# mLSTM of a hybrid encoder block: blocks of 128 tokens with a carried state in place of full 512x512 products

## The chip, the core and the metric

The kernel runs on one core of a Trainium2 chip, as one launch. The metric is the device time in microseconds (us). The engines have short names throughout: PE is TensorE (matrix products; PEld are its weight loads), ACT is ScalarE, DVE is VectorE, POOL is GpSimd, SP is SyncE, which issues most of the DMAs. SBUF is the working memory of 128 partitions; PSUM holds the results of PE in banks of 128 x 512 fp32.

## What is computed

The reference is one layer of an encoder on 512 tokens of width 1024, fp32 throughout. A normalised input goes through one wide projection; three mixers work on it (a bidirectional mLSTM, a 2-D neighbourhood attention, a cross-attention into 256 memory tokens), are merged by gates, projected and followed by a convolutional gated feed-forward network. The change concerns the mLSTM: 4 heads of 128 channels, run forwards and backwards and summed. Per direction the reference takes chunks of 64 tokens; inside a chunk it forms weighted scores, and between chunks it carries a state:

```python
C_new = decay[..., None, None] * C + jnp.einsum('bhl,bhld,bhle->bhde', wt, v_c, k_c)
n_new = decay[..., None] * n + jnp.einsum('bhl,bhle->bhe', wt, k_c)
...
P = jnp.exp(D - m_j[..., None]) * qk
inter_w = jnp.exp(inter_log - m_j)
num = jnp.einsum('bhcjs,bhcsd->bhcjd', P, v) + inter_w[..., None] * jnp.einsum('bhcde,bhcje->bhcjd', C_prev, q)
den = jnp.sum(P, axis=-1) + inter_w * jnp.einsum('bhce,bhcje->bhcj', n_prev, q)
h = num / jnp.maximum(jnp.abs(den), jnp.exp(-m_j))[..., None]
```

The size of a chunk is free in exact arithmetic: one chunk of 512 tokens without a state, and four chunks of 128 with one, give the same h. So do the stabilising maxima m, whatever they are, as long as they are used consistently.

## The kernel before

**Products.** Most products are done in a split form: an fp32 operand is cut into a high half (a copy in the type fp32r, by ACT) and a low half (the difference, by DVE), and `mm3` (lines 205 to 207) adds high x high, high x low and low x high. Weights arrive from DRAM as blocks of 512 KB on the SP queue, three blocks ahead, and are cut (`emit_split`, lines 187 and 188) one block ahead of their use. A few products, among them the mLSTM's values (line 603), take fp32 operands as they are; the text calls these unsplit.

**Order of the work.** The program is written against a framework of tiles: buffers come from pools of fixed size, and the framework places the semaphores and the order of each engine's queue, in which a later instruction can stand ahead of an earlier one. The main line is a row of projections (`proj`: 24 products of 512 columns for one 128-wide slice). The three mixers are written as generators; after each projection `step` lets the first unfinished one advance by 1.4 pieces on average in this part (0.75 in the projections of the memory tokens), so that a mixer's pieces stand between projections. PSUM has 4 banks for projections (`mmps`) and 4 for the mixers (`atps`).

**The mLSTM.** The queries and keys come out of a convolution (`conv`) and an activation (`silu2`, lines 398 to 403) and are cut into halves (`split_act`, lines 211 and 212) for use in `mm3`. `va` holds the values of all tokens and heads with a 129th column of constants, which yields the denominator. `ml_prep` works out the gates: cumulated log forget gates restarting at each block of 128 tokens (the scans), the running maximum m for each token and direction, `em` = exp(-m) (line 548), and `bi` (lines 550 to 558), the logarithmic weight of each source token relative to each later block, from the total decay `tot` of the blocks between. `R` (line 569, by DMA, spread to all partitions) holds the target's part; POOL adds the causal mask for the diagonal blocks (`rm`, line 572).

Per head `ml_all` then does:

- `kq_part` for each of four source blocks s: the scores of 128 source tokens to all 512 targets by `mm3`, and a copy into SBUF by ACT (line 581);
- `weights_J` for each of four target blocks J: five exponentials of 128x128 on ACT (line 591), for forward sources s = 0..J and backward sources s = J..3, and two products with the scores on DVE (lines 592 and 593);
- `values_J`: five unsplit products of the weights with `va` (line 603) into two columns groups of one PSUM bank, forward and backward; then the division by the denominator (lines 605 to 610) and the sum of squares (line 612);
- `normalise` and `emit_y`: the norm of the head, four transposes (line 627), the output gate, and a cut into halves for the branch's projection.

A piece ends at each `yield`: six per head. Values of block J-1 stand behind the weights of block J, values of block 3 in the next head's pieces.

The diff's functions stand here in full:

Of the kernel before, what the change touches and what calls it, by code (L numbers as in the profile page):

```python
# [11 lines left out]
F32 = mybir.dt.float32  # L12
# [92 lines left out]
def hybrid_block(ctx, tc, xg, xT, memT, wflat, vecs, gbias, nabias, outa, outb):  # L105
# [376 lines left out]
    def ml_prep():  # L482
        gv = Gt.rearrange("p t (d k h) -> p t d k h", d=2, k=2)
        T4 = lambda a: a.rearrange("p (t d h) -> p t d h", t=4, d=2)
        f = tiny(32)
        V.tensor_copy(T4(f), gv[:, :, :, 1, :])
        af = tiny(32)
        V.scalar_tensor_tensor(af, f, -1.0, f, op0=ALU.mult, op1=ALU.max)
        e = tiny(32)
        A.activation(e, af, AF.Exp, scale=-1.0)  # L490
        r = tiny(32)
        V.tensor_scalar(r, e, 2.0, None, op0=ALU.add)
        V.reciprocal(r, r)
# [48 lines left out]
        pmv = pm[:, :400].rearrange("p (t c) -> p t c", t=NT)  # L542
        for t in range(NT):
            PE.transpose(pmv[:, t, :], mr[:100, t * P:(t + 1) * P], ident[:100, :100])
# [3 lines left out]
        A.activation(em, pmv[:, :, 0:36], AF.Exp, scale=-1.0)  # L548
        tot = cp.tile([P, 4, 2, 4], F32, name="tot")
        V.tensor_copy(tot.rearrange("p t d h -> p (t d h)"), pt[:, :32])  # L550
        bi = cp.tile([P, 2, 4, 4, 4], F32, name="bi")
        for d in range(2):
            V.tensor_tensor(bi[:, d, 0], gv[:, :, d, 0, :], pmv[:, :, 64 + 32 * d:68 + 32 * d], op=ALU.subtract)
            for k in range(1, 4):
                if d == 0:
                    V.tensor_tensor(bi[:, 0, k, 0:4 - k], bi[:, 0, k - 1, 0:4 - k], tot[:, k - 1:3, 0, :], op=ALU.add)
                else:
                    V.tensor_tensor(bi[:, 1, k, k:4], bi[:, 1, k - 1, k:4], tot[:, 1:5 - k, 1, :], op=ALU.add)
        ml.update(rd=rd, em=em, bi=bi)

    def ml_all():
        yield from ml_prep()
        rd, em, bi = ml["rd"], ml["em"], ml["bi"]

        def load_R(h):
            R, rm = [], []
# [7 lines left out]
                rm.append(t)  # L574
            return R, rm

        def kq_part(h, kq, s):
            ps = atps()
            ks, qs = slice(h * S + s * P, h * S + (s + 1) * P), slice(h * S, (h + 1) * S)
            mm3(ps, kT[0][:, ks], kT[1][:, ks], qT[0][:, qs], qT[1][:, qs], True, True)  # L580
            A.activation(kq[:, s, :], ps, AF.Copy)

        def slots(J):
            return [(0, s) for s in range(J + 1)] + [(1, s) for s in range(J, NT)]

        def weights_J(h, J, R, rm, kq):
            js = slice(J * P, (J + 1) * P)
            E = tp.tile([P, 5, P], F32, tag="E", name=nm("E"))
            for i, (d, s) in enumerate(slots(J)):
                src = (rm if s == J else R)[d][:, js]  # L590
                A.activation(E[:, i, :], src, AF.Exp, bias=bi[:, d, abs(J - s), s, h:h + 1])  # L591
            V.tensor_tensor(E[:, 0:J + 1, :], E[:, 0:J + 1, :], kq[:, 0:J + 1, js], op=ALU.mult)
            V.tensor_tensor(E[:, J + 1:5, :], E[:, J + 1:5, :], kq[:, J:4, js], op=ALU.mult)
            return E

        def values_J(h, J, E, H, ss):
            js = slice(J * P, (J + 1) * P)
            ps = atps()
            pv = ps[:, :260].rearrange("p (d c) -> p d c", d=2)
            for d in range(2):  # L600
                lst = [(i, s) for i, (dd, s) in enumerate(slots(J)) if dd == d]
                for n, (i, s) in enumerate(lst):
                    PE.matmul(pv[:, d, 0:129], E[:, i, :], va[:, s, h, 0:129], start=n == 0, stop=n == len(lst) - 1)  # L603
# [32 lines left out]
        E = None  # L636
        R, rm = load_R(0)
        for h in range(4):
            kq = unit()[:, :4 * S].rearrange("p (s j) -> p s j", s=4)
            for s in range(2):  # L640
                kq_part(h, kq, s)
            yield
            if prev:
                values_J(h - 1, 3, E, *prev)
                normalise(*prev)
            for s in range(2, 4):
                kq_part(h, kq, s)
            yield
            H = tp.tile([P, S], F32, tag="H", name=nm("H"), bufs=4)
            ss = tiny(4)  # L650
            E = weights_J(h, 0, R, rm, kq)
            yield
            for J in range(1, NT):
                E2 = weights_J(h, J, R, rm, kq)
                if J == 3 and h < 3:
                    R, rm = load_R(h + 1)
                values_J(h, J - 1, E, H, ss)
# [5 lines left out]
        values_J(3, 3, E, *prev)  # L663
        normalise(*prev)
        yield
        emit_y(3, prev[0])
# [3 lines left out]
    def na_all(nq, nk, vw0, yh, yl):  # L670
# [55 lines left out]
        def transposes(i, sm):  # L726
# [3 lines left out]

            pp = []
            for bl in range(2):
                w = tp.tile([P, 5, P], F32R, tag="E", name=nm("w")).rearrange("p a b -> p (a b)")
# [3 lines left out]
                V.tensor_tensor(wv[:, :, 1, :], src, wv[:, :, 0, :].bitcast(F32), op=ALU.subtract)  # L737
                pp.append(w)
# [554 lines left out]
```

## Time and profile before

| what | value |
|---|---|
| median of 3 runs | 902.88 us (902.57 to 904.7) |
| the profiled execution's own time | 903.37 us |
| its span in the trace | 901.6 us |
| busy: PE, DVE, ACT, POOL | 894.5, 597.0, 466.9, 157.3 us |
| granted clock of PE, mean | 0.998 |
| instructions | 12452 |

All durations in the text come from the one profiled execution. Its span runs from the first to the last instruction in the trace; its own time is 1.8 us longer. In the listings a line begins with the source line (L603), the engine, the operation, "out<-in" by tile names, partitions x elements and a count; then come busy time and mean duration of one, and idle time of the engine before it with what ended it. A PE duration includes the time until its result has landed and overlaps with its successor's; what one product takes of PE is read from start to start, or from the chain of work that ended last, which has "start, us, what" in each row. Operands in fp32r are shown as f32. The mLSTM's pieces lie from about 108 to 255 us.

### The profile page before, as it was taken

What the parts mean: (1) busy time and instruction counts of PE and PEld (TensorE: products, weight loads), DVE (VectorE), ACT (ScalarE), POOL (GpSimd) and SP (SyncE); (2) the same over time, 40 slices, a digit from 0 to 9 for tenths busy, and PEclk for the clock granted to TensorE, in tenths of its full rate; (3) what the DMA queues carried; (4) which work ended last, traced back from release to release, by engine and by line L of the source; (5) the groups of instructions that cost most, each with busy time, mean ns of one, the idle gap of its engine ahead of it and who ended that gap; (6) DMA issues with size and microseconds to landing.
All of it is one profiled execution on the core that took longest, in us unless ns stands there. A gap on an engine that the chain in (4) does not pass through costs nothing.

```text
span 901.6 us, 12452 instructions
## 1 busy us (share of the span) xinstructions
PE 894.5 (99%) x4442; PEld 748.8 (83%) x4442; DVE 597.0 (66%) x1138; ACT 466.9 (52%) x983; POOL 157.3 (17%) x236
## 2 busy tenths in 40 slices
PE   9999999999999999999999999999999999999997
PEld 7899888888888888888888888888888888888887
DVE  6795676746666757998766547777733477777433
ACT  7474456656544647898734435444422344444442
POOL 5101231102070660420000211111100011111010
PEclk9999999999999999999999999999999999999999
DMA  7224633422252443443323422222232322222412
GB/s 263 101 72 134 200 135 97 162 93 94 71 138 74 116 126 121 136 134 118 117 89 107 144 97 96 94 97 96 65 98 95 117 95 94 94 93 89 129 41 94
DMA packets 39293, 99.69 MB, mean 111 GB/s; under 512 B 5688, under 2 KB 13624, under 8 KB 39232
## 3 DMA queue, kind: packets, MB, share of 16 engines
q1 hardware_dynamic: 31584, 92.39, 30.5%
q0 software_dynamic: 7360, 6.32, 3.2%
q8 instruction: 35, 0.57, 0.3%
q14 instruction: 26, 0.21, 0.1%
q10 hardware_dynamic: 288, 0.20, 0.1%
HBM read 94.67 MB, written 4.21 MB: 110 GB/s over the span
## 4 chain that ended last, share of the span: by engine, by line
PE 97%; ACT 1%; DMA 1%; issue 1%; SPq 0%; DVE 0%; POOLq 0%; POOL 0%; DVEq 0%
PE mm L205 28%; PE mm L207 28%; PE mm L206 28%; PE at L205 2%; PE at L206 2%; PE at L207 2%; PE at L603 2%; PE at L748 1%; PE at L729 1%; DMA wr<-wflat 1%; PE at L836 0%; PE at L711 0%; PE at L710 0%; ACT s L720 0%; PE at L290 0%
## 5 line engine op out<-in xcount | busy, mean ns | idle before, releaser
L205 PE MATMUL mm<-u,wh 128*128 128x512 f32 (+1 forms) x1076 | 419.8, 390 | 0.6 <-ACT wh L187 0.6
L206 PE MATMUL mm<-u,wh 128*128 128x512 f32 (+1 forms) x1076 | 417.4, 388 | 0.0
L207 PE MATMUL mm<-u,wl 128*128 128x512 f32 (+1 forms) x1076 | 416.9, 387 | 0.0
L187 ACT ACTIVATE wh<-wr 128x512 fp32r<-128x512 f32 (+1 forms) x298 | 186.0, 625 | 254.7 <-PE mm L206 214.0
L188 DVE TENSOR_TENSOR wl<-wr,wh 128x512 fp32r<-128x512 f32 (+3 forms) x299 | 229.6, 769 | 112.4 <-ACT wh L187 106.4
L207 PEld LDWEIGHTS mm<-u,wl 128*128 128x128 f32 x1076 | 202.1, 188 | 44.7 <-DVE wl L188 0.4
L205 PEld LDWEIGHTS mm<-u,wh 128*128 128x128 f32 x1076 | 202.1, 188 | 44.2 <-ACT wh L187 1.2
L206 PEld LDWEIGHTS mm<-u,wh 128*128 128x128 f32 x1076 | 202.3, 188 | 42.5 <-DVE u L212 0.3
L1162 POOL TENSOR_TENSOR s<-s,rb 128x512 f32<-128x512 f32 x22 | 29.2, 1328 | 266.9 <-DVE s L1161 258.8
L475 POOL DMA_DIRECT2D u<-nav_d x128 | 62.3, 503 | 75.0 <-PE at L748 34.1
L211 ACT ACTIVATE u<-s 128x512 fp32r<-128x512 f32 x34 | 21.5, 632 | 53.4 <-DVE s L1165 51.0
L212 DVE SCALAR_TENSOR_TENSOR u<-s,u 128x512 fp32r<-128x512 f32 x34 | 23.5, 692 | 14.9 <-ACT u L211 14.6
L1010 POOL TENSOR_TENSOR acc<-acc,s 128x512 f32<-128x512 f32 x7 | 9.1, 1300 | 129.7 <-ACT s L1009 129.7
L591 ACT ACTIVATE E<-R,bi 128x128 f32<-128x128 f32 x80 | 28.1, 396 | 5.6 <-POOL R L572 5.6
L393 ACT ACTIVATE s<-pad,vec 128x512 f32<-128x512 f32 x30 | 24.4, 815 | 8.3 <-DVE pad L391 8.3
L394 DVE SCALAR_TENSOR_TENSOR s<-pad,vec,s 128x512 f32<-128x512 f32 x30 | 22.5, 751 | 6.2 <-ACT s L393 6.1
L205 PE MATMUL mm<-wh,u 128*128 128x256 f32 (+1 forms) x80 | 24.5, 307 | 0.0
L206 PE MATMUL mm<-wl,u 128*128 128x256 f32 (+1 forms) x80 | 24.3, 304 | 0.0
L207 PE MATMUL mm<-wh,u 128*128 128x256 f32 (+1 forms) x80 | 24.3, 303 | 0.0
L1161 DVE SCALAR_TENSOR_TENSOR s<-s,s 128x512 f32<-128x512 f32 x22 | 15.2, 692 | 13.4 <-ACT s L1160 13.3
L391 DVE TENSOR_TENSOR pad<-mm,rb 128x512 f32<-128x512 f32 x22 | 15.1, 692 | 12.2 <-PE mm L207 12.2
L395 DVE SCALAR_TENSOR_TENSOR s<-pad,vec,s 128x512 f32<-128x512 f32 x30 | 22.5, 751 | 0.7
(282 smaller groups left out, 1049.7 us busy)
## 6 DMA issues: line engine op xcount, KB each, us to landing
wr<-wflat SPq DMA_DIRECT2D x140, 512.0 KB, 3.3
nab<-nabias SPq DMA_DIRECT2D x16, 256.0 KB, 2.7
u<-nav_d POOLq DMA_DIRECT2D x128, 32.0 KB, 2.6
s<-xT SPq DMA_DIRECT2D x15, 256.0 KB, 4.0
wr<-wflat SPq DMA_DIRECT2D x15, 192.0 KB, 2.4
nav_d<-nv POOLq DMA_DIRECT2D x8, 256.0 KB, 3.6
R<-rd SPq DMA_DIRECT2D x8, 256.0 KB, 3.4
wr<-wflat SPq DMA_DIRECT2D x2, 544.0 KB, 3.3
```

The costliest lines, as they stand in the source:

```text
L187: A.activation(h[:, u:v], src, AF.Copy)
L188: V.tensor_tensor(l[:, u:v], src, h[:, u:v].bitcast(F32), op=ALU.subtract)
L205: PE.matmul(ps, lh, rh, start=start, stop=False)
L206: PE.matmul(ps, lh, rl, start=False, stop=False)
L207: st["mm"] = PE.matmul(ps, ll, rh, start=False, stop=stop).ins
L212: V.scalar_tensor_tensor(l, src, scale, h.bitcast(F32), op0=ALU.mult, op1=ALU.subtract)
L393: A.activation(t1, pad[:, 0:512], AF.Identity, scale=vcol(w, i), bias=vcol(b, i))
L394: V.scalar_tensor_tensor(t1, pad[:, 1:513], vcol(w, n + i), t1, op0=ALU.mult, op1=ALU.add)
L395: V.scalar_tensor_tensor(t1, pad[:, 2:514], vcol(w, 2 * n + i), t1, op0=ALU.mult, op1=ALU.add)
L475: G.dma_start(vw[r * 32:(r + 1) * 32, i * 256:(i + 1) * 256], nav_v[hf, r, CW[b]:CW[b] + 32, hp * 256:(hp + 1) * 256])
L591: A.activation(E[:, i, :], src, AF.Exp, bias=bi[:, d, abs(J - s), s, h:h + 1])
L1162: G.tensor_tensor(c, c, rb2, op=ALU.mult)
```

## The change

The mLSTM is done in four blocks of 128 tokens, with a state carried from block to block in each direction.

- Queries and keys stay unsplit: `silu2` writes one fp32 tile, and its two cutting operations go, for eight tiles.
- `ml_prep`: the maximum at the last token of each block (first, backwards) is copied by ACT (`mc`) and spread to all partitions by two small products with a column of the identity (`mhp`); from it come `wt`, the weight of each token in the state at the end of its block, and `dec`, the decay of the state over a block; `bi` keeps its diagonal part only.
- `keys` (new): four transposes bring the head's keys to token-major order; ACT copies them (`kt`); DVE weights the values with `wt` (`wva`).
- `states` (new): per direction three unsplit products of keys and weighted values into one PSUM bank; the first state is copied by ACT, the next two are made by DVE with the decay.
- `weights_J`: only the diagonal block of scores is computed, as one unsplit product of 128x128 into the upper columns of the PSUM bank that later takes the values; two exponentials for the block itself, and one per direction that has a state, multiplied with the queries.
- `values_J`: per direction one product inside the block and one with the state.
- The tile `E` has four slots instead of five, also where the neighbourhood attention uses it.

The number of pieces per head stays six.

```diff
-        V.scalar_tensor_tensor(c, th, 1.0, c, op0=ALU.add, op1=ALU.mult)
-        split_act(dst[0][:, sl], dst[1][:, sl], c)
-    qT = [unit(F32R), unit(F32R)]
-    kT = [unit(F32R), unit(F32R)]
+        V.scalar_tensor_tensor(dst[:, sl], th, 1.0, c, op0=ALU.add, op1=ALU.mult)
+    qT, kT = unit(), unit()
...
+        mc = cp.tile([P, NT, 36], F32, name="mc")
+        A.activation(mc, pmv[:, :, 0:36], AF.Copy)
+        mhp = T4(pt[:, 64:96])
+        for d, e in ((0, P - 1), (1, 0)):
+            PE.matmul(mhp[:, :, d, :], ident[:, e:e + 1].to_broadcast([P, P]), mc[:, :, 32 * d:32 * d + 4],
+                      start=True, stop=True)
...
+            V.tensor_tensor(bi[:, d], gv[:, :, d, 0, :], pmv[:, :, 64 + 32 * d:68 + 32 * d], op=ALU.subtract)
+            V.tensor_tensor(wt[:, d], bi[:, d], tot[:, :, d, :], op=ALU.add)
+            V.tensor_tensor(dec[:, d], tot[:, 1:3, d, :], mh[:, 2 * d:2 * d + 2, d, :], op=ALU.add)
+        A.activation(wt, wt, AF.Exp)
+        A.activation(dec, dec, AF.Exp)
...
-        def kq_part(h, kq, s):
+        def keys(h):
+            pt = atps()
+            for J in range(NT):
+                PE.transpose(pt[:, J * P:(J + 1) * P], kT[:, h * S + J * P:h * S + (J + 1) * P], ident)
+            kt = scr()
+            A.activation(kt, pt, AF.Copy)
+            u = unit()
...
+            for d in range(2):
+                V.tensor_tensor(wva[:, d], va[:, d:d + 3, h, 0:129], wt[:, d, d:d + 3, h:h + 1].to_broadcast([P, 3, 129]),
+                                op=ALU.mult)
+            return kt, wva, C
+        def states(h, kt, wva, C):
+            for d in range(2):
+                ps = atps()
+                pc = ps[:, :387].rearrange("p (c e) -> p c e", c=3)
+                order = range(3) if d == 0 else range(2, -1, -1)
+                for i in order:
+                    PE.matmul(pc[:, i], kt[:, (i + d) * P:(i + d + 1) * P], wva[:, d, i], start=True, stop=True)
+                last = None
+                for i in order:
+                    if last is None:
+                        A.activation(C[:, d, i], pc[:, i], AF.Copy)
+                    else:
+                        V.scalar_tensor_tensor(C[:, d, i], C[:, d, last], dec[:, d, i + d - 1, h:h + 1], pc[:, i],
+                                               op0=ALU.mult, op1=ALU.add)
+                    last = i
+        def weights_J(h, J, R, rm):
+            js, hs = slice(J * P, (J + 1) * P), slice(h * S + J * P, h * S + (J + 1) * P)
             ps = atps()
...
-            mm3(ps, kT[0][:, ks], kT[1][:, ks], qT[0][:, qs], qT[1][:, qs], True, True)
-            A.activation(kq[:, s, :], ps, AF.Copy)
...
+            kq = ps[:, 384:512]
+            PE.matmul(kq, kT[:, hs], qT[:, hs], start=True, stop=True)
+            E = tp.tile([P, 4, P], F32, tag="E", name=nm("E"))
+            for d in range(2):
+                A.activation(E[:, d, :], rm[d][:, js], AF.Exp, bias=bi[:, d, J, h:h + 1])
+            ds = [d for d in range(2) if 0 <= J - 1 + 2 * d < NT]
+            for d in ds:
+                A.activation(E[:, 2 + d, :], R[d][:, js], AF.Exp, bias=mh[:, J - 1 + 2 * d, d, h:h + 1])
+            V.tensor_tensor(E[:, 0:2, :], E[:, 0:2, :], kq.unsqueeze(1).to_broadcast([P, 2, P]), op=ALU.mult)
+            a, b = 2 + ds[0], 3 + ds[-1]
+            V.tensor_tensor(E[:, a:b, :], E[:, a:b, :], qT[:, hs].unsqueeze(1).to_broadcast([P, b - a, P]), op=ALU.mult)
+            return E, ps
...
             for d in range(2):
-                lst = [(i, s) for i, (dd, s) in enumerate(slots(J)) if dd == d]
-                for n, (i, s) in enumerate(lst):
-                    PE.matmul(pv[:, d, 0:129], E[:, i, :], va[:, s, h, 0:129], start=n == 0, stop=n == len(lst) - 1)
+                inter = 0 <= J - 1 + 2 * d < NT
+                PE.matmul(pv[:, d, 0:129], E[:, d, :], va[:, J, h, 0:129], start=True, stop=not inter)
+                if inter:
+                    PE.matmul(pv[:, d, 0:129], E[:, 2 + d, :], C[:, d, J - 1 + d], start=False, stop=True)
...
         for h in range(4):
-            kq = unit()[:, :4 * S].rearrange("p (s j) -> p s j", s=4)
-            for s in range(2):
-                kq_part(h, kq, s)
+            st_h = keys(h)
             yield
             if prev:
-                values_J(h - 1, 3, E, *prev)
+                values_J(h - 1, 3, *E, C, *prev)
                 normalise(*prev)
-            for s in range(2, 4):
-                kq_part(h, kq, s)
+            states(h, *st_h)
+            C = st_h[2]
             yield
```

More of the change, by code (lines that the diff above doesn't have):

```diff
@@ L548, in ml_prep @@
         A.activation(em, pmv[:, :, 0:36], AF.Exp, scale=-1.0)
+        mc = cp.tile([P, NT, 36], F32, name="mc")
[4 more added lines that the diff above has]
+                      start=True, stop=True)
         tot = cp.tile([P, 4, 2, 4], F32, name="tot")
         V.tensor_copy(tot.rearrange("p t d h -> p (t d h)"), pt[:, :32])
-        bi = cp.tile([P, 2, 4, 4, 4], F32, name="bi")
-        for d in range(2):
[L553 to L559, printed above, removed]
+        mh = cp.tile([P, 4, 2, 4], F32, name="mh")
+        V.tensor_copy(mh.rearrange("p t d h -> p (t d h)"), pt[:, 64:96])
+        V.tensor_tensor(tot, tot, mh, op=ALU.subtract)
+        bi = cp.tile([P, 2, 4, 4], F32, name="bi")
+        wt = cp.tile([P, 2, 4, 4], F32, name="wt")
+        dec = cp.tile([P, 2, 2, 4], F32, name="dec")
+        for d in range(2):
+            V.tensor_tensor(bi[:, d], gv[:, :, d, 0, :], pmv[:, :, 64 + 32 * d:68 + 32 * d], op=ALU.subtract)
[3 more added lines that the diff above has]
+        A.activation(dec, dec, AF.Exp)
+        ml.update(rd=rd, em=em, bi=bi, mh=mh, wt=wt, dec=dec)
     def ml_all():
         yield from ml_prep()
-        rd, em, bi = ml["rd"], ml["em"], ml["bi"]
+        rd, em, bi, mh, wt, dec = [ml[n] for n in ("rd", "em", "bi", "mh", "wt", "dec")]
         def load_R(h):
@@ L575, in load_R @@
             return R, rm
-        def kq_part(h, kq, s):
-            ps = atps()
-            ks, qs = slice(h * S + s * P, h * S + (s + 1) * P), slice(h * S, (h + 1) * S)
-            mm3(ps, kT[0][:, ks], kT[1][:, ks], qT[0][:, qs], qT[1][:, qs], True, True)
[L581 to L586, printed above, removed]
-            js = slice(J * P, (J + 1) * P)
[L588 to L594, printed above, removed]
@@ L596, in values_J @@
-        def values_J(h, J, E, H, ss):
-            js = slice(J * P, (J + 1) * P)
-            ps = atps()
+        def keys(h):
[5 more added lines that the diff above has]
+            u = unit()
+            wva = u[:, :774].rearrange("p (d c e) -> p d c e", d=2, c=3)
+            C = u[:, 774:1548].rearrange("p (d c e) -> p d c e", d=2, c=3)
+            for d in range(2):
+                V.tensor_tensor(wva[:, d], va[:, d:d + 3, h, 0:129], wt[:, d, d:d + 3, h:h + 1].to_broadcast([P, 3, 129]),
+                                op=ALU.mult)
+            return kt, wva, C
@@ L650, in ml_all @@
             ss = tiny(4)
-            E = weights_J(h, 0, R, rm, kq)
+            E = weights_J(h, 0, R, rm)
             yield
             for J in range(1, NT):
-                E2 = weights_J(h, J, R, rm, kq)
+                E2 = weights_J(h, J, R, rm)
                 if J == 3 and h < 3:
                     R, rm = load_R(h + 1)
-                values_J(h, J - 1, E, H, ss)
+                values_J(h, J - 1, *E, C, H, ss)
                 E = E2
@@ L662, in ml_all @@
             prev = (H, ss)
-        values_J(3, 3, E, *prev)
+        values_J(3, 3, *E, C, *prev)
         normalise(*prev)
```

3 lines of the change are left out of this document (2 added, 1 removed).

## The prediction

> **What bounds the kernel now.** I read the page's busy shares first, then the chain of work that ended last, then what TensorE (PE) waited for.
>
> ```profile
> PE 894.5 (99%) x4442; PEld 748.8 (83%) x4442; DVE 597.0 (66%) x1138; ACT 466.9 (52%) x983; POOL 157.3 (17%) x236
> ...
> PE 97%; ACT 1%; DMA 1%; issue 1%; SPq 0%; DVE 0%; POOLq 0%; POOL 0%; DVEq 0%
> ```
>
> A busy PE alone proves little, because matmuls overlap in the trace. The chain is the better witness: 97% of the span is PE following PE. The view of waits, for PE alone, has three lines:
>
> ```profile
> PE at L235 <- PEq L1284: 0.8, 1, 0.8
> PE mm L205 <- ACT wh L187: 0.6, 2, 0.4
> PE at L748 <- DVE w L737: 0.2, 1, 0.2
> ```
>
> So PE lost 1.6 us to waits in 901.6 us, and none of it in the mLSTM. The kernel ends when PE has issued its products. What the change takes off PE is gained in full; what it takes off ScalarE (ACT), VectorE (DVE) or memory is worth nothing as long as PE does not begin to wait for them. How close they are in the mLSTM stretch is in the windows view (first number: PE busy; then weight loads, DVE, ACT, POOL):
>
> ```profile
> 120.00:135.00 15.00, 15.00 (x72) 12.26 (x70) 9.22 (x23) 8.83 (x23) 3.80 (x4) 1.00 0.41 142
> 135.00:165.00 30.00, 30.00 (x199) 27.26 (x199) 21.02 (x51) 20.16 (x57) 4.71 (x4) 1.00 0.33 106
> 165.00:195.00 30.00, 30.00 (x156) 25.34 (x155) 19.50 (x42) 19.64 (x55) 3.75 (x3) 1.00 0.42 141
> 195.00:220.00 25.00, 25.00 (x132) 21.02 (x131) 13.38 (x29) 13.15 (x42) 2.59 (x2) 1.00 0.31 106
> 220.00:250.00 30.00, 30.00 (x153) 25.30 (x154) 18.50 (x44) 16.32 (x47) 3.30 (x5) 1.00 0.20 71
> ```
>
> DVE works 9.22 + 21.02 + 19.50 + 13.38 + 18.50 = 81.6 of 130 us (63%), ACT 78.1 (60%), at a granted clock of 1.00. Both have room.
>
> **The price of one PE instruction.** I take prices from start to start, not from durations. The timeline of PE, then pieces of the chain, then a group by shape:
>
> ```profile
> 148.92 1.28 PE L603 MATMUL at<-u,E 128*128 128x129 f32 x10
> 149.95 0.47 PE L205 MATMUL at<-u,u 128*128 128x512 f32 x1
> 150.27 0.39 PE L206 MATMUL at<-u,u 128*128 128x512 f32 x1
> 150.49 0.39 PE L207 MATMUL at<-u,u 128*128 128x512 f32 x1
> 150.73 0.40 PE L205 MATMUL at<-u,u 128*128 128x512 f32 x1
> 150.96 0.40 PE L206 MATMUL at<-u,u 128*128 128x512 f32 x1
> 151.19 0.39 PE L207 MATMUL at<-u,u 128*128 128x512 f32 x1
> 151.43 0.28 PE L205 MATMUL mm<-u,wh 128*128 128x256 f32 x1
> ```
> ```profile
> 134.96 0.34 PE at L290 x4
> ...
> 149.08 1.12 PE at L603 x10
> ...
> 157.29 1.11 PE at L603 x10
> ...
> 166.61 0.44 PE at L627 x4
> ```
> ```profile
> L603 PE MATMUL at<-u,E 128*128 128x129 f32 x160 | 20.5, 275 | 0.0
> ```
>
> - One split score block is three products of 512 columns, L205 to L207: 150.73 to 151.43, 0.70 us. There are 16: 11.2 us.
> - The value products are unsplit fp32 already. Program text has 4 heads x 4 blocks x 5 = 80 of them and the trace 160, so an unsplit product is two instructions. Ten start within 149.95 - 148.92 = 1.03 us, 0.103 each. The product behind them takes 0.32 (to 150.27) where its successors take 0.23: a handover of 0.09. Together 1.11, as the chain has it. There are 16 groups: 17.8 us.
> - Four transposes cost 0.44 in the chain, 0.11 each.
>
> Before, then: 11.2 + 17.8 = **29.0 us** of PE in what the change rewrites.
>
> **After, on PE.** Per head, two instructions per unsplit product: four diagonal scores of 128x128 (8 instructions); 8 products inside a block plus 6 with the carried state, 14 in place of 20 (28 instructions); 6 state products of 129 columns (12); four transposes of the keys. Nothing in the trace is an unsplit product of 128 columns; L603 with 129 is its neighbour, so 0.103. In the order written, score J stands ahead of the values of J-1, which makes these groups per head, each with one handover:
>
> - score 0 alone: 2 x 0.103 + 0.09 = 0.29
> - score 1 with values 0 (6 instructions): 0.91
> - score 2 with values 1 (8), score 3 with values 2 (8): 1.11 each
> - values 3 (6) with the states (12): 1.94
> - transposes: 0.44
>
> That is 5.80, for four heads 23.2. Two small products that spread the running maximum of a block's last token come on top (4 instructions); the nearest row is L290 with four in 0.34. After: **23.5 us**, so 5.4 less. If no score shares a group with values, three more handovers per head add 1.0 and 4.4 is left. With no handover at all, 212 instructions x 0.103 = 21.8 leave 7.2. I take **5.0**, nearer to the groups as written, with something for groups that are split.
>
> A page of the Trainium skill speaks against unsplit fp32: "FP8 and Floating Point Precision", section TensorE Precision Notes, says that true fp32 takes four passes through the array. By that, an estimate, a product of 128 columns would cost as much as one 512-column pass, 0.23 in place of 0.206; 96 products would take 2.3 us more and the gain would be 2.7. The trace decides for two instructions in 0.206, and per 128x128 block the unsplit product is indeed dearer than a quarter of the split one (0.70 / 4 = 0.175); the gain comes from 16 blocks where there were 64.
>
> **Off PE.** Rows of the view by line, the second fence for DVE in the window 120 to 250:
>
> ```profile
> L591 ACT ACTIVATE E<-R,bi 128x128 f32<-128x128 f32 x80 | 28.1, 396 | 5.6 <-POOL R L572 5.6
> ...
> L581 ACT ACTIVATE u<-at 128x512 f32<-128x512 f32 x16 | 8.9, 597 | 0.0
> ```
> ```profile
> L592 DVE TENSOR_TENSOR E<-E,u 128x128 f32<-128x128 f32 (+3 forms) x16 | 9.8, 618 | 6.9 <-ACT u L581 4.1 <-ACT E L591 2.8
> L593 DVE TENSOR_TENSOR E<-E,u 128x512 f32<-128x512 f32 (+3 forms) x16 | 7.7, 485 | 1.2 <-ACT u L581 1.1
> L610 DVE SCALAR_TENSOR_TENSOR H<-at,y,H 128x128 f32<-128x128 f32 x16 | 5.6, 350 | 4.8 <-ACT H L609 4.7
> ...
> L914 DVE TENSOR_TENSOR u<-mm,rb_m 128x256 f32<-128x256 f32 x4 | 1.7, 421 | 0.1
> ```
>
> - ACT: 56 exponentials in place of 80 (-9.5 us), 4 key copies in place of 16 score copies (-7.2), 8 copies of a first state of about 0.35, the size of L610's block (+2.8): -13.9. Worth nothing, ACT is covered.
> - DVE: L592 and L593 go (-17.5). In come 16 products of 128x256 with the scores read from PSUM (L914: 0.421, 6.7), 16 with the queries, half of them 128x256, half about 0.3 (5.8), 8 weightings of values of 387 columns (L593's 384 wide ones stand between 0.42 and 0.69; say 0.56, 4.5), 16 state steps of 128x129 (L610: 0.350, 5.6): 22.6, so +5.1 and about 1 of small ones. DVE goes from 63% to 70% of its stretch. PE covers it.
> - The splits of queries and keys (eight on ACT, eight on DVE) go. By the view of waits PE did not wait for them: nothing.
> - DMA: the same rows of R are loaded, no issue is added; two 128x2064 buffers are freed. Nothing.
>
> **Waits that come in.** Three chains are new. (a) Scores are no longer computed ahead: the product goes to PSUM, DVE multiplies (0.42), multiplies again (0.42), then PE takes the values. With the product's own 0.275 some 1.2 us with two hand-overs between engines. (b) Keys: transposes, a copy on ACT (0.597), the states: about 1.0. DVE's weighting (0.56) runs beside it. (c) The running maximum has to be copied by ACT behind the exponential before PE can spread it:
>
> ```profile
> 120.28 1.14 ACT L187 ACTIVATE wh<-wr 128x512 fp32r<-128x512 f32 x2
> 120.33 0.51 PE L544 MATMUL at<-ident,s 100*128 100x100 f32 x4
> ...
> 121.32 0.27 ACT L548 ACTIVATE em<-at 128x144 f32<-128x144 f32 x1
> ```
>
> ACT stood behind two splits of weights until 121.3, so the copy would have ended at 121.9, 1.1 us after PE was through with the four transposes at 120.84. Each is paid in full only if PE has nothing else in its queue. Between two pieces of the mLSTM stands as a rule one projection, 24 products x 0.23 = 5.5 us. And where a product isn't ready, others already stand in its place in the queue; the timeline of PE shows it in the score blocks of the last head:
>
> ```profile
> 218.63 0.39 PE L207 MATMUL at<-u,u 128*128 128x512 f32 x1
> 218.87 0.39 PE L205 MATMUL mm<-u,wh 128*128 128x512 f32 x1
> 219.10 0.39 PE L206 MATMUL mm<-u,wh 128*128 128x512 f32 x1
> 219.32 0.39 PE L207 MATMUL mm<-u,wl 128*128 128x512 f32 x1
> 219.55 0.40 PE L205 MATMUL mm<-u,wh 128*128 128x512 f32 x1
> 219.83 0.50 PE L205 MATMUL at<-u,u 128*128 128x512 f32 x1
> ```
>
> Four products of the projection fill the time between the third score block and the fourth, which had no PSUM bank yet. I therefore cost these waits at zero, with ends 0 and what rival A gives. Behind a DVE multiply that waits for its score stand the low halves of the next weights; they run about a block ahead, and the score is the first product after the projection that DVE waits for anyway. That adds nothing, and up to 0.3 us per piece without the cover.
>
> **Sum.** The profiled execution has a span of 901.6 and took 903.37, so 1.8 lie outside; that stays. 903.37 - 5.0 = 898.4. It lies 0.5 above the median of the runs, 902.88, from which the forecast is **897.9 us**, 0.55% less. About 0.3% (2.7 us) is what a measurement here can tell from no change.
>
> **Rivals.**
>
> A, slower: the values stand directly behind their own scores in PE's queue. A step takes 1.4 pieces per projection, so 0.4 of 1.4, or about 5 of the 16 values, come without a projection between; 5 x 1.2 + 4 x 1.0 for the states + 1.1 for the maximum = 11.1 us of waiting, against 5.0 gained: 909.0. It decides from 7.7 us of waits on. For it: these chains are new, and before every score was a step or more ahead. Against it: the filled gap at 218.87, and no wait of PE in 130 us before. 7%.
>
> B, no difference: only the states and the maximum are uncovered, 4 x 1.0 + 1.1 = 5.1, and the gain is eaten: 903.0. For it: each is one chain without a spare step for head 0. Against it: the same filling. 8%.
>
> C, the change doesn't shorten PE as counted: small instructions hold the array for their whole duration. The row of L603 has 275 ns; if the 16 transposes cost that, they take 4.4 in place of 1.8, the gain falls to 2.4, and the time is 900.5. The Trainium skill ("TensorE: Matmul & The Clock Gate", Part 4) gives a transpose about 275 ns in a kernel; the row agrees as a duration, but four of them in 0.44 us speak against it as a price. 5%.
>
> D, the forecast: 80%.
>
> **Chances and range.** Faster by over 0.3% is D, 0.80; within 0.3% are B and C, 0.13; slower is A, 0.07. The range runs from 895.6 (no handovers, gain 7.2, rounded to 895.5) to 901.0, which takes in C and some 2.5 us of waits above the gain of 4.4, and leaves A and B out.
>
> **What would show it.** Score products of 128 columns at 0.103 per instruction; values groups of 6 to 10 instructions; the chain still 97% PE; the waits of PE for E, the key copy or the maximum's copy below 1 us together. PE waits at the values line above 3 us, or handovers well over 0.09 in front of the new small groups, would make me wrong. So would weights that come late: then a wait for wl or wh appears in the same stretch.

## The result, and the profile after

The changed kernel takes **898.05 us** (median of 6 runs, 896.86 to 899.74) against 902.87 (6 runs, 902.57 to 904.7) for the kernel before: a ratio of 0.9943, 95% interval 0.9929 to 0.9956. That is 0.57% less time; 897.9 us was forecast. Run again beside other kernels it took 897.39, ratio 0.9938 (0.9926 to 0.9951). The profiled execution took 899.74, the slowest of its six, with a span of 898.0.

The busy row and the chain row of the page of after:

```profile
PE 890.3 (99%) x4446; PEld 747.2 (83%) x4446; DVE 579.5 (65%) x1154; ACT 451.6 (50%) x950; POOL 165.2 (18%) x236
...
PE 95%; DMA 1%; ACT 1%; DVE 1%; issue 1%; POOL 0%; SPq 0%; POOLq 0%; DVEq 0%
```

PE still sets the end, though the chain has a few links on other engines now. The waits of PE in after (engine and line, what it waited for; total, times, longest):

```profile
PE at L608 <- DVE u L597: 0.8, 1, 0.8
PE at L235 <- PEq L1321: 0.8, 1, 0.8
PE mm L205 <- ACT wh L187: 0.5, 1, 0.5
```

The second and third stood there before. The first is new: once, 0.8 us, the state products for the weighted values. What PE does in the mLSTM, in groups by shape:

```profile
L640 PE MATMUL at<-u,E 128*128 128x129 f32 x64 | 11.8, 276 | 0.0
L642 PE MATMUL at<-u,E 128*128 128x129 f32 x48 | 9.3, 275 | 0.0
L608 PE MATMUL at<-u,s 128*128 128x129 f32 x48 | 6.2, 278 | 0.8 <-DVE u L597 0.8
L623 PE MATMUL at<-u,u 128*128 128x128 f32 x32 | 6.0, 275 | 0.0
L590 PE MATMUL at<-ident,u 128*128 128x128 f32 x16 | 2.4, 275 | 0.0
...
L552 PE MATMUL at<-mc,ident 128*128 128x16 f32 x4 | 0.6, 268 | 0.0
```

64 + 48 + 48 + 32 + 16 + 4 = 212 instructions, as counted. The busy sums overlap and are no prices; those come from the chain of after (start, us, what):

```profile
152.30 0.44 PE at L590 x4
...
158.44 0.22 PE at L640 x2
...
159.11 1.34 PE at L608 x12
```

An unsplit product, two instructions, advances the chain by 0.22 us; twelve take 1.34, 0.112 each; a transpose takes 0.11.

**Where the time went.** I measure on PE from start to start, between instructions that both kernels have: from the first four transposes of the gates to the last head's transposes (the mLSTM stretch). In the timeline of before, then of after:

```profile
108.83 0.60 PE L515 MATMUL at<-ident,lfc 128*100 128x128 f32 x4
...
252.30 0.60 PE L627 MATMUL at<-ident,H 128*128 128x128 f32 x4
```
```profile
110.16 0.60 PE L513 MATMUL at<-ident,lfc 128*100 128x128 f32 x4
...
249.69 0.60 PE L666 MATMUL at<-ident,H 128*128 128x128 f32 x4
```

143.47 us before, 139.53 after. The wait at L608 lies in it; a second profile of after has no such wait, and there the stretch is 138.77. The first products start 108.83 and 110.16 us into the span: after lost 1.3 us before the mLSTM began. And there is the tail, from the last product of `KS` and `QS` in the neighbourhood attention to the last transposes of the kernel; not one instruction in it was changed. Its first and last row in PE's timeline, in before (its second profile) and after (its second):

```profile
435.45 0.28 PE L710 MATMUL at<-KS,QS 128*128 128x256 f32 x1
...
895.35 0.38 PE L1084 MATMUL mm<-ident,u 128*128 128x128 f32 x2
```
```profile
430.88 0.28 PE L747 MATMUL at<-KS,QS 128*128 128x256 f32 x1
...
889.62 0.38 PE L1121 MATMUL mm<-ident,u 128*128 128x128 f32 x2
```

The tail takes 459.9 us there and 458.7 here. The first profiles have the same two lengths. Over the profiled executions: -3.9 in the mLSTM, -1.2 in the tail, +1.3 at the start, +0.2 between: -3.6, which is 903.37 to 899.74.

| kernel | mLSTM stretch begins | its length | tail |
|---|---|---|---|
| before, two profiles | 108.83, 108.20 | 143.47, 143.48 | 459.9, 459.9 |
| after, two profiles | 110.16, 108.27 | 139.53, 138.77 | 458.7, 458.7 |
| whole scores unsplit | 108.11 | 146.02 | 458.9 |
| split diagonal | 108.15 | 142.83 | 458.8 |
| states twice | 110.23 | 144.22 | 458.8 |
| splits kept | 110.01 | 138.42 | 458.8 |
| state weights first | 107.99 | 138.58 | 458.7 |
| no lag | 108.68 | 142.73 | 458.9 |
| scores ahead | 109.72 | 138.36 | 458.8 |
| before, shifted | 115.20 | 143.40 | 460.7 |
| after, shifted | 114.44 | 138.61 | 460.8 |

So the gain has an intended part, 4.7 us in the mLSTM (second profiles), and one that nothing in the change asked for. The two shifted kernels, explained below, show the first part alone: their tails are alike, and the stretch is again 4.8 us shorter in after.

### The profile page after: what moved, and what is told of

Same layout as the page of the kernel before. It is cut to its first block, busy times and chain, and to the rows that moved or that the text cites. A ratio compares the mean times of both kernels' runs of the same rounds, so it can differ in the third digit from the quotient of the medians.

```text
span 898.0 us, 12449 instructions
## 1 busy us (share of the span) xinstructions
PE 890.3 (99%) x4446; PEld 747.2 (83%) x4446; DVE 579.5 (65%) x1154; ACT 451.6 (50%) x950; POOL 165.2 (18%) x236
## 4 chain that ended last, share of the span: by engine, by line
PE 95%; DMA 1%; ACT 1%; DVE 1%; issue 1%; POOL 0%; SPq 0%; POOLq 0%; DVEq 0%
PE mm L206 28%; PE mm L205 28%; PE mm L207 28%; PE at L205 2%; PE at L206 2%; PE at L207 2%; PE at L785 1%; PE at L640 1%; PE at L766 1%; PE at L608 1%; PE at L642 1%; DMA R<-rd 1%; DMA wr<-wflat 0%; PE at L623 0%; PE at L873 0%
## 5 line engine op out<-in xcount | busy, mean ns | idle before, releaser
L188 DVE TENSOR_TENSOR wl<-wr,wh 128x512 fp32r<-128x512 f32 (+3 forms) x299 | 212.6, 712 | 113.2 <-ACT wh L187 108.5
L1199 POOL TENSOR_TENSOR s<-s,rb 128x512 f32<-128x512 f32 x22 | 36.9, 1676 | 258.2 <-DVE s L1198 250.1
L211 ACT ACTIVATE u<-s 128x512 fp32r<-128x512 f32 x26 | 16.4, 631 | 53.5 <-DVE s L1202 53.2
L1202 DVE TENSOR_TENSOR s<-mm,s 128x512 f32<-128x512 f32 x22 | 15.2, 689 | 21.4 <-POOL s L1199 21.4
L212 DVE SCALAR_TENSOR_TENSOR u<-s,u 128x512 fp32r<-128x512 f32 x26 | 18.0, 692 | 14.3 <-ACT u L211 14.1
L1197 ACT ACTIVATE s<-s 128x512 f32<-128x512 f32 x22 | 13.9, 632 | 15.6 <-DVE s L1196 15.5
```

The source lines that it names most:

```text
L188: V.tensor_tensor(l[:, u:v], src, h[:, u:v].bitcast(F32), op=ALU.subtract)
L211: A.activation(h, src, AF.Copy, scale=scale)
L212: V.scalar_tensor_tensor(l, src, scale, h.bitcast(F32), op0=ALU.mult, op1=ALU.subtract)
L1199: G.tensor_tensor(c, c, rb2, op=ALU.mult)
```

## The experiments

My theory: PE's instructions are the gain (16 blocks of scores for 64), the unsplit form saves nothing by itself, and everything off PE is free. The rivals: the gain comes from the cheaper form or from the splits that go; or waits eat a good part of it; or small instructions are dearer than counted.

**Only the unsplit form.** The kernel before, with queries and keys as one fp32 tile each and the whole 512-column scores unsplit:

```diff
-    qT = [unit(F32R), unit(F32R)]
-    kT = [unit(F32R), unit(F32R)]
+    qT, kT = unit(), unit()
...
-            mm3(ps, kT[0][:, ks], kT[1][:, ks], qT[0][:, qs], qT[1][:, qs], True, True)
+            PE.matmul(ps, kT[:, ks], qT[:, qs], start=True, stop=True)
```

> The kernel before with one part of the change alone: queries and keys stay unsplit, and the 16 score blocks of 512 columns are one unsplit product each; no carried state. It computes the whole reference. Counting theory (PE's products set the time, ACT and DVE are covered): an unsplit product is two instructions, and 0.103 us at 129 columns scales to 0.41 at 512, so 0.82 in place of 0.70, 16 x 0.12 = +1.9 us against before, 904.8; taking the eight splits off ACT and DVE gives nothing. Rival (part of the gain came from the work taken off ACT and DVE): below before, 901 to 902.5.

Measured: 904.07 us, ratio to before 1.0015 (1.0006 to 1.0025). A piece of its chain of work:

```profile
150.16 1.72 PE at L578 x4
```

Two products of 512 columns take 1.72 us, so 0.86 each where the split form took 0.70: 16 x 0.16 = 2.6 more, and the stretch grew by 2.5. That is the price alone; the time grew by only 1.1 since the tail became 1.0 shorter, as in after. Unsplit scores are a loss at 512 columns, so the gain cannot come from the form at that size.

**The diagonal blocks in the split form.** After, with each 128x128 score done by three split products, their halves cut per block:

```diff
-            PE.matmul(kq, kT[:, hs], qT[:, hs], start=True, stop=True)
+            hl = tp.tile([P, S], F32R, tag="H", name=nm("hl"), bufs=4).rearrange("p (a b) -> p a b", a=4)
+            split_act(hl[:, 0, :], hl[:, 1, :], kT[:, hs])
+            split_act(hl[:, 2, :], hl[:, 3, :], qT[:, hs])
+            mm3(kq, hl[:, 0, :], hl[:, 1, :], hl[:, 2, :], hl[:, 3, :], True, True)
```

> The kernel after, but the diagonal score block of 128x128 is done in the split form, three products in place of one unsplit; the halves are made per block by two more ACT and two more DVE instructions of 128x128. It computes the whole reference. Counting theory: if an instruction of 128 columns never takes less than the 0.103 us of its weight load, 3 x 0.103 in place of 2 x 0.103, 16 x 0.103 = +1.6 us against after, 899.7. If the split product is paid by its columns (0.23 / 4 = 0.06 each), 3 x 0.06 in place of 0.206, -0.4 us, 897.6. Rival (ACT and DVE matter): 32 more instructions on each, some 11 us of ACT and 9 of DVE, would show as +3 us or more, with PE waits on the halves.

Measured: 900.92 us, ratio to before 0.9975 (0.9965 to 0.9985), about 3 more than after; the stretch is 4.1 longer than in the second profile of after. The timeline of PE, then the waits:

```profile
135.51 0.28 PE L206 MATMUL at<-hl 128*128 128x128 f32 x1
135.62 0.27 PE L207 MATMUL at<-hl 128*128 128x128 f32 x1
135.73 0.28 PE L205 MATMUL at<-hl 128*128 128x128 f32 x1
```
```profile
PE at L608 <- DVE u L597: 0.7, 1, 0.7
PE at L643 <- DVE E L633: 0.4, 2, 0.2
PE at L552 <- ACT mc L549: 0.3, 1, 0.3
```

Split products of 128 columns start 0.11 apart, as far as unsplit instructions do; three in place of two make 16 x 0.11 = 1.8. The three waits make 1.4, and some 0.9 is spread over smaller gaps. ACT and DVE each have 32 more cuts to make here, two ahead of every score, but only the 0.4 us at L643 is new: a wait at L608 stands in the first profile of after, and one of 0.2 at L552 in "no lag" and "scores ahead". How much of the rest the cuts make is not shown. The time came nearer to the rival's 3 us than to the 1.6 of the counting, so "everything off PE is free" holds for the change as written and not for any amount of work on ACT and DVE. At 128 columns an instruction costs 0.11 whatever its type; of the two sizes measured, unsplit is the cheaper form at 128 alone. With the scores split, 1.8 of the 5.4 us that the count gives for the change would be gone.

**The states twice.** After, with each state product issued two times into the same columns:

```diff
-                    PE.matmul(pc[:, i], kt[:, (i + d) * P:(i + d + 1) * P], wva[:, d, i], start=True, stop=True)
+                    for _ in range(2):
+                        PE.matmul(pc[:, i], kt[:, (i + d) * P:(i + d + 1) * P], wva[:, d, i], start=True, stop=True)
```

> The kernel after, with each of the 24 state products issued twice, the second over the first; 48 more instructions of 129 columns on PE and nothing else. It computes the whole reference. Counting theory: 48 x 0.103 = +4.9 us against after, 903.0, as slow as before. Rival (PE has slack in this stretch, the gain is from elsewhere): +1 us or less.

Measured: 902.86 us, ratio to before 0.9999 (0.9990 to 1.0008), 5.5 above the second measurement of after; the stretch is 5.45 longer. A row of this kernel's chain:

```profile
159.84 2.68 PE at L609 x24
```

24 instructions in 2.68, 12 in 1.34: 0.112 for each one added, with nothing over. 48 of them make 5.4 us, and all of it is in the time: PE's small instructions are paid in full, at 0.112.

**The splits kept.** After, with the eight cuts of queries and keys still made, by ACT and DVE, and used by nobody:

```diff
         V.scalar_tensor_tensor(dst[:, sl], th, 1.0, c, op0=ALU.add, op1=ALU.mult)
+        hl = [sp.tile([P, 516], F32R, tag="scr", name=nm("s"))[:, :S] for _ in range(2)]
+        split_act(hl[0], hl[1], dst[:, sl])
```

> The kernel after, with the eight splits of queries and keys put back (eight ACT copies and eight DVE differences of 128x512, 5.0 and 5.5 us), their results unused. It computes the whole reference. Counting theory: no difference to after, 898.0 within 0.5. Rival (the work taken off ACT and DVE gave part of the gain): +1 to +2.5 us.

Measured: 897.78 us, ratio to before 0.9941 (0.9927 to 0.9954), no different from after. The cuts cost nothing, so their removal gave nothing.

**The wait at the first states.** In after the chain shows whence it came:

```profile
118.96 2.75 DMA rd<-s
...
121.72 5.08 DMA R<-rd
...
126.87 1.30 POOL R L581
...
128.20 0.70 ACT E L626 x2
128.89 0.13 ACT wt L566
...
129.04 0.79 DVE u L597
```

ACT's queue held the exponentials of the first weights (L626), which need R through two DMAs and POOL's mask, ahead of the exponential that makes `wt`, which needs none of them. DVE's weighting and the states stood behind. The kernel that mends it places the weights of block 0 behind `wt` and `dec`:

```diff
-        A.activation(dec, dec, AF.Exp)
+        st["dec"] = A.activation(dec, dec, AF.Exp).ins
...
-            E = weights_J(h, 0, R, rm)
+            with tc.issue_after(st["dec"]):
+                E = weights_J(h, 0, R, rm)
```

> The kernel after, with the first head's exponentials for block 0 queued on ACT behind the two small exponentials of the state weights and decays; nothing else. It computes the whole reference. In the profile after, PE waited once in the mLSTM: 0.84 us at the first state products, for DVE's weighted values, which waited for ACT, where an exponential stood ahead that waited for the R rows by DMA and POOL. Queue theory (the order on ACT makes this wait): it goes, -0.8 to -1.0 us against after, 897.1. Rival (the states wait for something else as well, or the saved time is lost to the next wait): within 0.3 us of after.

Measured: 896.61 us, ratio to before 0.9926 (0.9913 to 0.9939): the best version, 0.7% less than before. The wait is gone from its profile and the stretch is 138.58. How much of that the edit earned stays open: one of two profiles of after lacks the wait as well, and the intervals overlap.

**No lag.** After, with the values of a block directly behind its own weights (rival A made whole):

```diff
-            E = weights_J(h, 0, R, rm)
+            values_J(h, 0, *weights_J(h, 0, R, rm), C, H, ss)
             yield
             for J in range(1, NT):
-                E2 = weights_J(h, J, R, rm)
+                E = weights_J(h, J, R, rm)
...
-                values_J(h, J - 1, *E, C, H, ss)
-                E = E2
+                values_J(h, J, *E, C, H, ss)
```

> The kernel after, with the values of a block issued in the same piece as its weights and scores, instead of one piece later. It computes the whole reference. Forecast's view (PE's queue puts ready products of the projection ahead of the values, so the chain score, DVE, values is covered): within 1 us of after, at most 899. Rival A of the prediction (values behind their own scores make PE wait some 1.2 us each): 16 x 1.2 = +19 us, 917; half of it where a projection happens to stand between.

Measured: 901.62 us, ratio to before 0.9984 (0.9975 to 0.9993): 4.2 more than the second measurement of after, between the two expectations. The waits of PE, then DVE, POOL and PE in the timeline at the second:

```profile
PE at L308 <- DVE s L307: 1.2, 1, 1.2
PE at L640 <- DVE E L630: 1.1, 1, 1.1
...
PE at L608 <- DVE u L597: 0.7, 1, 0.7
```
```profile
172.99 1.29 POOL L581 TENSOR_TENSOR R<-R,msk 128x512 f32<-128x512 f32 x1 [0.41 <-DMA R<-rd]
173.05 1.78 DVE L212 SCALAR_TENSOR_TENSOR u<-s,u 128x512 fp32r<-128x512 f32 x1
...
175.35 0.41 DVE L630 TENSOR_TENSOR E<-E,at 128x256 f32<-128x256 f32 x1
...
175.82 0.49 PE L640 MATMUL at<-u,E 128*128 128x129 f32 x2 [1.12 <-DVE E L630]
```

Only one of 16 blocks of values shows a wait. Two cuts in a row stood ahead of it on DVE (L188 from 171.34 on, then L212) and took 1.78 us each, where a cut of this size takes 0.69 in after, while POOL worked on its masks. L308 belongs to the norm of the memory tokens, which this order put in PE's way. L608 is not the wait known from after, at the first states: here it stands at 218.7 us, at the states of the last head. With one of 0.2 at L552 the waits come to 3.1 us, and the stretch is 4.0 longer than in the second profile of after. Even without the lag, projection products take the place of most values that aren't ready.

**Scores ahead.** The order of "state weights first", and the four diagonal scores of a head in one PSUM bank behind the states, copied to SBUF by ACT, so that DVE finds every score ready:

```diff
+        def scores(h):
+            ps = atps()
+            for J in range(NT):
+                hs = slice(h * S + J * P, h * S + (J + 1) * P)
+                PE.matmul(ps[:, J * P:(J + 1) * P], kT[:, hs], qT[:, hs], start=True, stop=True)
+            kq = scr()
+            A.activation(kq, ps, AF.Copy)
+            return kq
...
-            kq = ps[:, 384:512]
-            PE.matmul(kq, kT[:, hs], qT[:, hs], start=True, stop=True)
+            kq = kq4[:, js]
```

> The kernel after with the order on ACT of the run before it, and the four diagonal scores of a head in one group of eight instructions behind the states, copied to SBUF by ACT (0.6 us per head); the weights read the copy. It computes the whole reference. Counting theory: the same 212 instructions, up to three handovers of 0.09 less per head, at most -1.0 us beside the 0.8 to 1.0 of the run before, 896.1 to 897.1. Rival (small groups on PE aren't where time is left): the same as the run before it.

Measured: 896.92 us, ratio to before 0.9932 (0.9920 to 0.9944); the stretch is 138.36, within 0.2 of "state weights first". Neither the earlier scores nor fewer, larger groups gain anything that shows: no wait for a score was left to remove, and no handover to save.

**The tail.** Before, unchanged, measured once more, and then both kernels with one more buffer taken ahead of the first one, so that the buffers behind it may lie elsewhere:

```diff
+    z = unit()
+    G.memset(z[:, 0:1], 0.0)
     hx = [unit(F32R) for _ in range(4)]
```

> The kernel before, unchanged, for a second trace of it. In its first trace the stretch from the neighbourhood attention to the last instruction took 459.9 us from the first key product of that attention on, and in the traces of after and of six variants 458.7 to 458.9, although the order on all engines is the same there. If that belongs to the kernel (where its buffers lie), it is 459.9 again; if it was that one execution, it is 458.8. The time: 902.9, ratio 1.000.

> The kernel before with one unused large buffer taken and given back ahead of the first (one memset of a column on POOL), so that the large buffers of the whole kernel may lie elsewhere; the order of the work is the same. It computes the whole reference. Placement theory: the last stretch moves from 459.9, towards 458.8 or past it, -1 us in the time at most. Rival (the 1 us came from one execution or from the order): 459.9 as in the kernel before, or the same as in its second trace.

> The kernel after with the same unused buffer taken and given back first. It computes the whole reference. Placement theory: the last stretch moves from 458.7, +1 us at most. Rival: 458.7 as in all variants of after. The mLSTM stretch stays at 138.4 to 139.6 under both.

Measured: 902.89 us for before (0.9998, 0.9989 to 1.0006), 910.28 shifted (1.0078, 1.0066 to 1.0091), and 906.19 for after shifted (1.0036, 1.0022 to 1.0050). Most of the shift's cost is at the start, and is the edit's own; the waits of before, shifted:

```profile
PE mm L375 <- ACT u L329: 5.7, 1, 5.7
```

The length of the tail belongs to the kernel and not to one execution: both profiles of before have 459.9. It is 460.7 and 460.8 us in the two shifted kernels: after lost 2.1 us there, and before 0.8. Behind the start, after shifted has the same instructions in the same order on every engine as after. What goes with the length of the tail is in the view by line, from 550 to 870 us, of before (second profile), after (second profile) and after shifted:

```profile
L188 DVE TENSOR_TENSOR wl<-wr,wh 128x512 fp32r<-128x512 f32 (+1 forms) x119 | 99.7, 838 | 43.9 <-ACT wh L187 41.9
L1162 POOL TENSOR_TENSOR s<-s,rb 128x512 f32<-128x512 f32 x22 | 29.1, 1324 | 266.9 <-DVE s L1161 258.9 <-issue 8.1
```
```profile
L188 DVE TENSOR_TENSOR wl<-wr,wh 128x512 fp32r<-128x512 f32 (+1 forms) x117 | 82.8, 708 | 44.2 <-ACT wh L187 42.6
L1199 POOL TENSOR_TENSOR s<-s,rb 128x512 f32<-128x512 f32 x21 | 35.1, 1673 | 246.5 <-DVE s L1198 238.4 <-issue 8.1
```
```profile
L188 DVE TENSOR_TENSOR wl<-wr,wh 128x512 fp32r<-128x512 f32 (+1 forms) x119 | 98.5, 828 | 43.6 <-ACT wh L187 41.5
L1201 POOL TENSOR_TENSOR s<-s,rb 128x512 f32<-128x512 f32 x22 | 29.6, 1345 | 267.1 <-DVE s L1200 259.1 <-issue 8.1
```

On the mean either DVE's cut of a weight is slow (0.83 to 0.84 us) and POOL's product quick (1.32 to 1.35), or the cut is quick (0.69 to 0.71) and the product slow (1.67 to 1.72). In all 13 profiles the first goes with a tail of 459.9 to 460.8 and the second with 458.7 to 458.9. Where POOL's products run (550 to 640 and 720 to 830 us), PE's 512-column products start 0.2319 us apart in before, 0.2328 and 0.2325 in the two shifted kernels, and 0.2309 in after; between 650 and 710 us, without them, all lie within 0.2310 and 0.2314.

Which of the two is slow does not set PE's pace, though. In the first profile of after POOL's product starts first here and there, and the cut is the slow one:

```profile
717.80 1.29 POOL L1199 TENSOR_TENSOR s<-s,rb 128x512 f32<-128x512 f32 x1 [70.90 <-DVE s L1198]
717.83 1.81 DVE L188 TENSOR_TENSOR wl<-wr,wh 128x512 fp32r<-128x512 f32 x1
```

From this product to the next of POOL's, 48 products of PE start 0.2308 apart, just as behind the one at 739.98, where the cut takes 0.69 and POOL 1.85. The pattern of DVE and POOL is a mark of the longer tail and not its cause.

With order and instructions the same, what sets after shifted apart from after is where the buffers may lie (the traces hold no addresses), and a start 4 to 6 us later; starts that differ by 2 us among the other kernels go with no difference in the tail. I take it for the buffers' place, which is argued and not shown. Of the parts of the change, "whole scores unsplit" has the two freed buffers but not the carried state, and its tail is 458.9 as well. So the freed memory is the likely reason for the shorter tail; how a buffer's place would slow PE stays open.

## Why the prediction was right, and where it wasn't

- **PE is the bound, and what leaves PE is gained in full.** Right: 5.4 us of products put in (states twice) cost 5.5, and the eight cuts, an instruction on ACT and one on DVE each (splits kept), cost 0.
- **0.103 us per unsplit instruction and 0.09 per handover.** The sum was right and the split wrong. An instruction costs 0.112 and there is no handover: the twelve added by "states twice" cost as much as the first twelve. The row of ten had 1.12 in all, and the 0.09 at its end, booked as a handover, is part of the ten. 212 x 0.112 = 23.7, against 23.5. The bound of 7.2 (0.103, no handover) was therefore out of reach; as an end of the range it gives 902.88 - 7.2 = 895.7, not the 895.6 that stands there.
- **The four passes for unsplit fp32.** 0.22 per product of 129 columns and 0.86 at 512 are measured. The Trainium skill ("FP8 and Floating Point Precision", TensorE Precision Notes) has four passes for true fp32; against a split product's 0.23 at 512 columns that is an estimate of 0.92 at 512 and 0.23 at 128, and the trace agrees within 7%. It was the prediction's use of it that failed: it charged the price by the Trainium skill to the 96 new products, and left the 80 old ones, which are unsplit as well, at 0.103. With 0.112 per instruction on both sides before costs 11.2 + 160 x 0.112 = 29.1, and the difference is 5.4.
- **Gain on PE 5.0.** The stretch lost 4.7 in the second profile of after, 4.9 with the state weights first, 5.1 with the splits kept. Of the 5.4 by count, 0.3 to 0.7 stays unlocated.
- **ACT and DVE worth nothing.** Right. From 108 to 255 us, before and then after (PE, weight loads, DVE, ACT, POOL):

```profile
108.00:255.00 147.00, 147.00 (x783) 125.12 (x782) 96.14 (x210) 85.68 (x235) 23.97 (x25) 1.00 0.32 107
```
```profile
108.00:255.00 147.00, 146.16 (x804) 124.74 (x803) 100.29 (x237) 76.54 (x212) 27.74 (x33) 1.00 0.33 113
```

  ACT lost 9.1 us there and DVE took on 4.2, less than the 13.9 and 6 counted, partly since the window holds some 4 us more of other work in after. Over the whole span DVE fell by 17.5 us, from 597.0 to 579.5; some 16 of them are the quicker cuts between 550 and 870 us, which the change did not touch. PE is busy for 146.16 of 147: the 0.84 us are the one wait.
- **The new waits cost nothing.** Nearly: the score's chain (a) and the copy of the maximum (c) show no wait in after; (c) shows one of 0.2 to 0.3 us in three variants (split diagonal, no lag, scores ahead). The prediction's (b) took the keys' copy for the late link and DVE's weighting for work beside it; late was the weighting, because the exponential for `wt` stood in ACT's queue behind two that waited for R, an order that the step left out. 0.8 us, in one profile of two.
- **"two 128x2064 buffers are freed. Nothing."** This is the term that failed: whatever its cause, an effect outside the rewritten part was put at nothing, and the tail, with unchanged instructions, is 1.2 us shorter. The freed buffers are the likely reason, not a shown one. With it the total came out where it was forecast, 4.8 to 5.5 less, from 4.7 + 1.2 minus up to 1 of wait and up to 2 at the start. That the forecast was hit to 0.2 us is partly luck.
- **Rival A** fell by its own kernel: without the lag the stretch grows by 4.0 us, with 1.1 us of waiting at one value and none at the other 15, not 16 x 1.2, so filling works. The loss would still be most of the gain. **B** would have needed 5.1 us of waits, and there were 0.8. **C** fell in after's chain: four transposes in 0.44, though each lasts 275 ns.

## What to carry to other kernels

Price an edit on the bounding engine by instructions, and take the price from a chain row whose count differs, not from one group: 12 in 1.34 and 24 in 2.68 give 0.112, where a single group gave 0.103 and a handover that isn't there. Use the unsplit form for blocks of 128 columns (0.22 against 0.33 for three split products) and the split form for 512 (0.70 against 0.86). And compare the stretches that a change does not touch before the gain is put down to it: here a fifth of it came from there.

## What the runs showed of the hardware that was not expected

**DVE and POOL hold each other up.** A cut of 128x512 that takes 0.69 us took 1.78 beside POOL's mask (no lag, above), and in the tail one of the two is always the slow one. The Trainium skill ("SBUF — State Buffer", Who interferes with whom) says that a VectorE instruction with two inputs in SBUF and a GpSimd instruction that reads SBUF share a pair of ports, that one locks the other out for its whole length, and that the order of issue decides which. The trace agrees on all three: the cut that starts 0.03 us behind POOL's product (717.83, above) ends 0.55 us after it, and where the cut starts no later, at 739.98, it takes 0.69 and the product 1.85. The same section has it that PE waits on nobody. The trace does not speak against that: PE's products kept 0.2308 us whether DVE or POOL was held up.

**The first products can run at little over half speed.** In the first profile of after, and then in the second:

```profile
6.78 0.63 PE L206 MATMUL mm<-u,wh 128*128 128x512 f32 x1
7.20 0.63 PE L205 MATMUL mm<-u,wh 128*128 128x512 f32 x1
```
```profile
6.38 0.39 PE L206 MATMUL mm<-u,wh 128*128 128x512 f32 x1
6.62 0.39 PE L205 MATMUL mm<-u,wh 128*128 128x512 f32 x1
```

Starts 0.42 us apart in one and 0.24 in the other, from the same kernel; in the first this goes on for nine products: up to 2 us of difference that no edit caused, though the windows view gives both a granted clock of 1.00 from 6 to 12 us. The Trainium skill ("TensorE: Matmul & The Clock Gate", Part 1) describes a half rate until TensorE has been busy for a window of some 3.4 us that runs freely, so that the same kernel sees more or fewer slow products. That the slow products come and go fits. But in the first profile they last until 9.8 us, 9 us after PE's first product, longer than one such window, and the granted clock does not show them; so the cause is not shown here.
